# A 3x3 convolution with 2x2 max pooling on one core: the opening's order changed, one cast moved from ScalarE to VectorE

## The chip, the cores and the metric

The kernel runs on one core of one Trainium2 chip. The metric is the device time of one execution in microseconds (us); lower is better. Three executions of the kernel before took 104.12, 104.49 and 104.11 us, a median of 104.12 us. A core has five engines with a queue each: TensorE (PE, with its weight loads listed apart as PEld), VectorE (DVE), ScalarE (ACT), GpSimd (POOL) and SyncE (SP, which here only issues transfers). An engine takes its instructions strictly in the order of its own queue, and waits on semaphores for the others.

## The reference

The input x has 16 images of 64 channels, 64 by 64; the weight has 128 output channels. The convolution pads with one row and column of zeros; then the maximum of each 2x2 block is taken.

```python
x_pad = np.pad(x, ((0, 0), (0, 0), (1, 1), (1, 1)), mode='constant')
conv[b, co] += weight[co, ci, kh, kw] * x_pad[b, ci, kh:kh+64, kw:kw+64]   # over ci, kh, kw
output[b, c, i, j] = np.max(conv[b, c, 2*i:2*i+2, 2*j:2*j+2])              # 16 x 128 x 32 x 32, float32
```

## The kernel before, in words

**Tiling.** Two images make a pair: 2 x 64 channels fill the 128 partitions. Every pair is cut into 4 quarters of 16 input rows (8 output rows), which gives 32 steps. A step makes, for each of its two images (halves h = 0 and 1), one block of 128 output channels x 8 output rows x 64 columns. A product of 64 input channels uses half of the TensorE array, so two products, one on each half, run side by side; the kernel always issues them in such pairs (`product`, two lanes, L248).

**Algorithm.** The two convolution rows 2i and 2i+1 of a pooling window are not made one by one. With weight rows g0, g1, g2, one accumulator (`ta`) holds the part in which the two rows differ and another (`tb`) the part from which the maximum follows: VectorE takes the maximum of `tb` and the copied `ta` (MX, L427), and a last product that both rows share is added to it (PR for K steps, P1 for W steps). Each product is three matmuls, one for each column of the 3x3 window, onto one of eight PSUM banks.

**Two kinds of steps** (L37). K steps (0, 2, 5, 7, 10, ...) read the image as bf16 in `kx`. Their products are PA1 and PA2 (into `ta`), PB1 and PB2 (into `tb`) and PR (of `ks`, the sum of two rows, made on VectorE by KS, L296). W steps (1, 3, 4, 6, ...) read float32 rows in `wx`; GpSimd or VectorE makes the difference of two rows (E, L344) and the difference of rows one apart (D, L353), VectorE the sum (WS); products P2 (of E, into `ta`), P0 and P3 (of D), P1 (of WS). After the products ScalarE copies `ta` to SBUF (EV, L411 and L413), which frees the bank, VectorE takes MX, ScalarE copies odd columns (OD, L431), and VectorE takes the column maximum (CM, L437), which frees the `tb` bank; SP stores the result. For a W step, SE (L423) copies `ta` into the `tb` bank first.

**The opening.** SP loads, in this order: the weights; the first chunk of image pair 0 in two parts (`kfirst`); the rows of step 1 in two parts (`wx`); the chunk of step 2 (`ksecond`, L123). Weights are made as D0, D2, G0, G1, G2, GM and GP (`wq`), turned on TensorE by transposes (TD0 ... TGP, L164) and copied out of PSUM by VectorE or ScalarE (VD0 ... VGP, L175 to L181). The chunks of `kfirst` are cast to bf16 by VectorE (XEa, XOa, XOb, XEb, L453). The chunk of step 2 is cast by `cast_more` (L455): X1 casts the 8 rows 17, 19, ..., 31, X2 the 8 rows between them; both on ScalarE (L460), since `CAST_ON_VECTOR` is empty. PA1 and PA2 of step 2 read only odd rows, PB1 and PB2 only even rows, KS.2 all of them. The products of step 0 are cut in halves (F, products 0 to 3), those of step 1 too (G.k.part: G.0 the product P2, G.1 the product P0, G.2 the product P3), and the differences of step 1 are made in halves by VectorE (Ea, Eb) and GpSimd (Da, Db, L380).

**Chunks 3 and 4 of image pair 0** are loaded by GpSimd itself, cast by the DMA on the way: LK.0.0 (rows 33 to 48, read by step 5) and LK.0.1 (rows 49 to 63, read by step 7), both L98. They stand in GpSimd's queue in the order LK.0.0, Da, Db, LK.0.1, D.3, E.4, ...

**What sets the order.** The order is written out by hand, in the string `ORDER`; no scheduler moves anything. Every name in it appends its instructions to the queues of their engines. Beside the data dependencies there is one more rule (L76 to L82): a GpSimd operation made through `on_gpsimd` also waits for the last VectorE operation that was made through `on_vector` (casts, weight differences, KS, Ea and Eb) ahead of it in `ORDER`. LK.0.1 has no such wait of its own; it only stands behind what is ahead of it in GpSimd's queue. A PSUM bank is handed out from a queue of free ones, in the order of `ORDER`.

```python
def on_vector(inst):
    sbuf_op[0] = inst
    return inst

def on_gpsimd(inst):
    behind(inst, sbuf_op[0])
    return inst
```

Of the kernel before, what the change touches and what calls it, by code (L numbers as in the profile page):

```python
# [11 lines left out]
def kernel(  # L12
# [23 lines left out]

    TYPES = "KWKWWKWKWWKWWKWKWWKWWKWWWWKWWKWW"  # L37
    DIFF_ON_VECTOR = (3, 8, 14,)
    CAST_ON_VECTOR = ()
    SUM_BY_REDUCTION = (1, 3, 4, 11, 12, 14, 16, 17, 19, 20, 25, 30,)  # L40

    FROM_BANK = (6,)
# [33 lines left out]
# [3 lines that stand above are left out]
# [59 lines left out]
    D0, G2, D2, G0, G1, GM, GP = BLOCKS.values()  # L138
# [7 lines left out]
    g0, g1, g2 = wv[:, 0:3, :], wv[:, 3:6, :], wv[:, 6:9, :]  # L146
# [308 lines left out]
    def cast_more(first):  # L455
        dst, src = kx[0][:, klo2 + first : khi2 : 2, :], ksecond[:, first::2, :]
        if first in CAST_ON_VECTOR:
            on_vector(nc.vector.tensor_copy(out=dst, in_=src))
# [30 lines left out]
    for m in PRODUCTS:  # L489
        steps[m] = lambda s, h, m=m: product(m, s, h)  # L490

    ORDER = """
        D0 g2 TD0 g0 D2 GS TG2 g1 VD0 PR.0.1 XEa TD2 VG2 PA1.2.1 TG0 F.2.0 VD2 XOa LB.3 LB.4 LB.6 LB.8 LB.9 GM
        VG0 F.3.0 XOb F.0.0 F.1.0 TGM TG1 F.0.1 PA2.2.1 XEb LK.0.0 F.1.1 F.2.1 F.3.1 VGM GP Ea KS.0 Eb VG1
        EV.0.1 G.0.0 EV.0.0 G.0.1 P2.3.1 SE.1.0 SE.1.1 MX.0.1 Da Db TGP MX.0.0 VGP LK.0.1 X2 PR.0.0 G.1.0 X1
        G.2.0 PB1.2.1 PB2.2.1 WS.1 G.2.1 G.1.1 L.11 P0.3.1 PA1.2.0 PA2.2.0 P3.3.1 OD.0.0 OD.0.1 EV.1.0 E.3 KS.2
        CM.0.1 EV.1.1 P1.1.1 D.3 CM.0.0 PR.2.1 PB1.2.0 P2.3.0 PA1.5.1 PA2.5.1 MX.1.0 EV.2.0 MX.1.1 L.12 L.14
        WS.3 EV.2.1 E.4 SE.3.1 P1.1.0 PB2.2.0 SE.3.0 D.6 P2.4.1 OD.1.0 P0.3.0 MX.2.1 CM.1.0 EV.3.1 MX.2.0
        P3.3.0 PA1.5.0 EV.3.0 MX.3.1 WC.6 OD.1.1 D.4 MX.3.0 PA2.5.0 CM.1.1 PR.2.0 OD.2.1 P1.3.0 CM.2.1 E.6
# [91 lines left out]
```

## Time and profile before

| what | value |
|---|---|
| median of three executions | 104.12 us (104.11 to 104.49) |
| the profiled execution, its own time | 104.27 us |
| its span in the profile | 102.5 us, 2534 instructions |
| PE busy | 96.0 us (94%), 908 matmuls |
| DVE busy | 92.7 us (90%), 179 instructions |
| ACT busy | 81.5 us (80%), 180 instructions |
| POOL busy | 74.8 us (73%), 61 instructions |
| granted TensorE clock | 1.0 throughout |
| HBM traffic over the span | 17.14 MB read, 8.39 MB written |

The 104.27 us are the span and 1.77 us around it. Times below are in us from the span's start. An engine's busy share is an average over the span, and a matmul counts as busy until its modelled end, so that PE busy says little by itself; what counts is whether PE's matmuls follow each other without a gap, and what ended the gaps there are. In the view of the timeline a line is a run of like instructions: start, duration, engine, line, operation, tiles, shapes, count, and in brackets the idle time of the engine ahead of it and what ended it.

### The profile page before, as it was taken

How to read it: one execution, taken by the hardware profiler on the slowest of the kernel's cores; microseconds unless marked ns; L12 is line 12 of the kernel's file. 1: busy time of each engine (PE TensorE's matmuls, PEld its weight loads, DVE VectorE, ACT ScalarE, POOL GpSimd, SP SyncE). 2: the span in 40 equal slices, each digit the busy share in tenths (PEclk: the TensorE clock that was granted, in tenths of full speed). 3: DMA queues.
4: the chain of work that ended last, by engine and by line, in shares of the span. 5: the costliest groups of instructions: out<-in, count | busy, mean ns of one | idle time of the engine just before them, and what ended most of it. 6: DMA issues, size and time to landing. Idle time of an engine off the chain costs nothing.

```text
span 102.5 us, 2534 instructions
## 1 busy us (share of the span) xinstructions
PE 96.0 (94%) x908; PEld 55.7 (54%) x908; DVE 92.7 (90%) x179; ACT 81.5 (80%) x180; POOL 74.8 (73%) x61
## 2 busy tenths in 40 slices
PE   6889899999999999999999999999999999999920
PEld 2367655556865566566666667455444444444400
DVE  1497999999999899999999999999799899999970
ACT  5537988699699979978676999797898899897740
POOL 6128589997796889998999699668969967950000
PEclk9999999999999999999999999999999999999999
DMA  2999999999999999929999993023996522113244
GB/s 52 330 352 310 356 287 269 385 404 232 163 233 386 389 360 348 357 75 195 217 293 387 384 355 132 6 102 123 213 218 200 203 71 102 58 45 107 104 166 142
DMA packets 13421, 23.34 MB, mean 228 GB/s; under 512 B 1120, under 2 KB 9568, under 8 KB 13408
## 3 DMA queue, kind: packets, MB, share of 16 engines
q1 hardware_dynamic: 12400, 20.68, 59.4%
q0 software_dynamic: 864, 2.36, 13.3%
q8 instruction: 7, 0.11, 0.4%
q10 hardware_dynamic: 144, 0.13, 0.4%
q14 instruction: 6, 0.05, 0.1%
HBM read 17.14 MB, written 8.39 MB: 249 GB/s over the span
## 4 chain that ended last, share of the span: by engine, by line
PE 87%; DVE 5%; DMA 3%; issue 1%; DVEq 0%
PE acc L195 86%; DMA wraw<-in_weight_dram 3%; DVE acc L427 2%; DVE o L437 1%; PE acc L164 1%; DVE kx L453 1%; DVE wq L467 0%; DVE wt L181 0%; DVEq L586 0%; DVEq L427 0%
## 5 line engine op out<-in xcount | busy, mean ns | idle before, releaser
L195 PEld LDWEIGHTS <-wt 64*128 64x128 bf16 x876 | 53.3, 94 | 37.9 <-issue 1.8
L353 POOL TENSOR_TENSOR wd<-wx 128x1024 bf16<-128x1024 f32 x20 | 47.0, 2362 | 6.5 <-DVE ws L330 3.1
L195 PE MATMUL acc<-wd,wt 64*128 64x504 bf16 (+3 forms) x264 | 51.3, 367 | 0.0
L195 PE MATMUL acc<-kx,wt 64*128 64x504 bf16 (+6 forms) x288 | 48.5, 356 | 0.4 <-DVE kx L453 0.4
L427 DVE TENSOR_TENSOR acc<-acc,ev 128x512 f32<-128x512 f32 x64 | 41.8, 691 | 1.9 <-PE acc L195 0.8
L195 PE MATMUL acc<-we,wt 64*128 64x512 bf16 (+2 forms) x132 | 31.8, 367 | 0.0
L195 PE MATMUL acc<-ws,wt 64*128 64x504 bf16 (+1 forms) x126 | 30.7, 377 | 0.0
L413 ACT ACTIVATE ev<-acc 128x512 f32<-128x512 f32 x42 | 24.8, 605 | 3.6 <-PE acc L195 3.4
L423 ACT COPY acc<-acc 128x512 f32<-128x512 f32 x42 | 24.5, 589 | 3.8 <-PE acc L195 1.5
L431 ACT COPY od<-acc 128x256 f32<-128x256 f32 x64 | 22.8, 378 | 4.7 <-PE acc L195 4.4
L437 DVE TENSOR_TENSOR o<-acc,od 128x256 f32<-128x256 f32 x64 | 24.9, 414 | 1.0 <-ACT od L431 0.9
L344 POOL TENSOR_TENSOR we<-wx 128x512 bf16<-128x512 f32 x16 | 20.3, 1272 | 4.0 <-DVE ks L296 1.7
L195 PE MATMUL acc<-ks,wt 64*128 64x504 bf16 (+1 forms) x66 | 15.9, 377 | 0.5 <-DVE acc L427 0.5
L322 DVE TENSOR_REDUCE ws<-wx 128x512 bf16<-128x1024 f32 x12 | 14.7, 1229 | 0.0
L411 ACT COPY ev<-acc 128x512 f32<-128x512 f32 x22 | 12.4, 595 | 0.9 <-PE acc L195 0.8
L330 DVE TENSOR_TENSOR ws<-wx 128x512 bf16<-128x512 f32 x8 | 5.6, 708 | 0.0
L98 POOL DMA_DIRECT2D kx<-in_x_dram x6 | 3.5, 587 | 1.8 <-DVE kx L453 1.8
L296 DVE TENSOR_TENSOR ks<-kx 128x512 bf16<-128x512 bf16 x11 | 4.7, 442 | 0.0
L548 PE MATMUL acc<-const-bfloat16-1.0 128*128 128x512 bf16 x8 | 3.3, 585 | 0.8 <-PEq L572 0.8
L467 DVE TENSOR_TENSOR wq<-wraw 128x192 bf16<-128x192 f32 x1 | 0.5, 499 | 2.7 <-DMA wraw<-in_weight_dram 2.7
L380 POOL TENSOR_TENSOR wd<-wx 128x512 bf16<-128x512 f32 x2 | 2.5, 1262 | 0.5 <-DVE we L365 0.5
L468 POOL TENSOR_TENSOR gsum<-wraw 128x192 f32<-128x192 f32 x1 | 0.8, 812 | 2.7 <-DVE wq L466 2.7
(31 smaller groups left out, 21.9 us busy)
## 6 DMA issues: line engine op xcount, KB each, us to landing
out_dram<-o SPq DMA_DIRECT2D x26, 256.0 KB, 5.9
wx<-in_x_dram SPq DMA_DIRECT2D x10, 512.0 KB, 8.2
wx<-in_x_dram SPq DMA_DIRECT2D x5, 544.0 KB, 10.1
wx<-in_x_dram SPq DMA_DIRECT2D x5, 480.0 KB, 9.6
out_dram<-o SPq DMA_DIRECT2D x11, 128.0 KB, 2.0
kx<-in_x_dram POOLq DMA_DIRECT2D x2, 528.0 KB, 8.3
ksecond<-in_x_dram SPq DMA_DIRECT2D x1, 512.0 KB, 5.7
kx<-in_x_dram POOLq DMA_DIRECT2D x2, 256.0 KB, 8.4
```

What stands on the lines that cost most here:

```text
L195: nc.tensor.matmul(acc[t][:, i0:i1, o0:o1], wt[lo : lo + CI, m0 + kw - h, :], rows(lo, i0, i1, c0, c1), start=start and kw == 1, stop=True ...
L296: nc.vector.tensor_tensor(out=row["ks", s], in0=t[:, f : f + 2 * R : 2, :], in1=t[:, f + 1 : f + 2 * R : 2, :], op=ADD)
L322: nc.vector.tensor_reduce(out=row["ws", s], in_=t[:, f : f + 2 * R, :].rearrange("p (r two) w -> p r w two", two=2), axis=mybir.AxisListTy ...
L330: nc.vector.tensor_tensor(out=row["ws", s], in0=t[:, f : f + 2 * R : 2, :], in1=t[:, f + 1 : f + 2 * R : 2, :], op=ADD)
L344: inst = (nc.vector if vector else nc.gpsimd).tensor_tensor(out=row["we", s], in0=t[:, f : f + 2 * R : 2, :], in1=t[:, f + 1 : f + 2 * R : ...
L353: nc.gpsimd.tensor_tensor(out=row["wd", s], in0=t[:, f + 1 : f + 1 + 2 * R, :], in1=t[:, f - 1 : f - 1 + 2 * R, :], op=SUB)
L411: nc.scalar.copy(out=ev[s, h], in_=acc[t])
L413: nc.scalar.mul(ev[s, h], acc[t], -1.0)
L423: nc.scalar.copy(out=acc[t], in_=acc[ta[s, h]])
L427: nc.vector.tensor_tensor(out=t, in0=t, in1=ev[s, h], op=MAX)
L431: nc.scalar.copy(out=od[s, h], in_=acc[tb[s, h]][:, :, 1::2])
L437: nc.vector.tensor_tensor(out=ot[s][:, h], in0=acc[t][:, :, 0::2], in1=od[s, h], op=MAX)
```

## The change

Three things are changed, all in the opening.

1. `CAST_ON_VECTOR` becomes `(0,)`: X1 (odd rows of step 2's chunk) is issued on VectorE at L458 through `on_vector`, instead of on ScalarE. In `ORDER` it moves from behind G.1.0 to a place ahead of EV.0.1, and thus ahead of Da and Db. In VectorE's queue it stands behind VGP and ahead of MX.0.1. Da is now ordered behind X1, where it was ordered behind Eb.
2. The products PA1 and PA2 of step 2 (both halves) stand ahead of PR of step 0 in TensorE's queue. Before, they stood behind G.1 and G.2 of step 1. In the old string the half h = 1 of PR.0 stood first in its lane; the pairs themselves are the same ones.
3. TGP, the four transposes of GP, moves from behind G.0 to a place between F.2.1 and F.3.1; VGP moves with it on VectorE, from behind MX.0.0 to a place behind VG1.

With that TensorE's queue in the opening reads (before) F.3.1, G.0.0, G.0.1, TGP, PR.0, G.1.0, G.2.0, G.2.1, G.1.1, PA1.2, PA2.2, PB1.2.0 with P2.3.1, and (after) TGP, F.3.1, G.0.0, G.0.1, PA1.2, PA2.2, PR.0, G.1.0, G.2.0, G.1.1, G.2.1, PB1.2.0 with P2.3.1. From there on the order is the same. VectorE has one instruction more and ScalarE one less. The queues of GpSimd and SP hold the same instructions in the same order. The PSUM banks of some steps change places.

```diff
-    CAST_ON_VECTOR = ()
+    CAST_ON_VECTOR = (0,)
...
-        D0 g2 TD0 g0 D2 GS TG2 g1 VD0 PR.0.1 XEa TD2 VG2 PA1.2.1 TG0 F.2.0 VD2 XOa LB.3 LB.4 LB.6 LB.8 LB.9 GM
-        VG0 F.3.0 XOb F.0.0 F.1.0 TGM TG1 F.0.1 PA2.2.1 XEb LK.0.0 F.1.1 F.2.1 F.3.1 VGM GP Ea KS.0 Eb VG1
-        EV.0.1 G.0.0 EV.0.0 G.0.1 P2.3.1 SE.1.0 SE.1.1 MX.0.1 Da Db TGP MX.0.0 VGP LK.0.1 X2 PR.0.0 G.1.0 X1
-        G.2.0 PB1.2.1 PB2.2.1 WS.1 G.2.1 G.1.1 L.11 P0.3.1 PA1.2.0 PA2.2.0 P3.3.1 OD.0.0 OD.0.1 EV.1.0 E.3 KS.2
+        D0 g2 TD0 g0 D2 GS TG2 g1 VD0 XEa TD2 VG2 TG0 F.2.0 VD2 XOa LB.3 LB.4 LB.6 LB.8 LB.9 GM VG0 F.3.0 XOb
+        F.0.0 F.1.0 TGM TG1 F.0.1 XEb LK.0.0 GP F.1.1 F.2.1 TGP F.3.1 VGM Ea KS.0 Eb VG1 VGP X1 EV.0.1 G.0.0
+        EV.0.0 G.0.1 SE.1.0 SE.1.1 PA1.2.1 PA1.2.0 PA2.2.1 PA2.2.0 MX.0.1 Da Db MX.0.0 LK.0.1 PR.0.1 PR.0.0
+        P2.3.1 G.1.0 X2 G.2.0 PB1.2.1 PB2.2.1 WS.1 G.1.1 G.2.1 L.11 P0.3.1 P3.3.1 OD.0.0 OD.0.1 EV.1.0 E.3 KS.2
```

## The prediction

> **What bounds the kernel now.** I read the chain that ended last first. After an opening of about 10 us it is one piece of PE:
>
> ```profile
> 9.36 1.31 DVE acc L427 x2
> 10.67 0.04 issue
> 10.71 85.77 PE acc L195 x801
> ```
>
> 801 matmuls in 85.77 us, that is 0.214 us for each pair, the pace of a pair of 512 columns in the rows below. So from 10.71 us on PE hardly waits, and the end is PE's start plus its work plus a tail. Whatever delays PE after 10.71 us is paid in full; whatever starts it earlier is gained only if every operand comes earlier too. Next, PE's timeline in the opening and at step 7's first product:
>
> ```profile
> 7.76 1.49 PE L195 MATMUL acc<-kx,wt 64*128 64x256 bf16 x24
> 9.08 0.82 PE L195 MATMUL acc<-we,wt 64*128 64x256 bf16 x12
> 9.83 0.40 PE L164 MATMUL acc<-ident,wq 128*128 128x128 bf16 x4
> 10.71 0.82 PE L195 MATMUL acc<-ks,wt 64*128 64x512 bf16 x6 [0.48 <-DVE acc L427]
> 11.35 1.49 PE L195 MATMUL acc<-wd,wt 64*128 64x256 bf16 x24
> 12.67 1.67 PE L195 MATMUL acc<-kx,wt 64*128 64x512 bf16 x13
> ...
> 20.45 0.38 PE L195 MATMUL acc<-kx,wt 64*128 64x512 bf16 x1
> ```
>
> In order: the last half of F; G.0; TGP; PR.0 after a wait of 0.48 us for MX.0 (the only one that the change can remove); G.1 and G.2; PA1.2, PA2.2 and PB1.2.0; at 20.45 PA1.7.0. Third, the weight loads, which run ahead of their matmuls and so show waits that PE itself does not yet feel:
>
> ```profile
> 17.79 0.61 PEld L195 LDWEIGHTS <-wt 64*128 64x128 bf16 x8 [0.25 <-DMA kx<-in_x_dram]
> ...
> 20.32 0.69 PEld L195 LDWEIGHTS <-wt 64*128 64x128 bf16 x8 [0.19 <-DMA kx<-in_x_dram]
> ```
>
> Twice the load ahead of a matmul waits for an image transfer by GpSimd: at 17.79 for LK.0.0 (step 5), at 20.32 for LK.0.1 (step 7). The matmuls follow at 17.85 and 20.45, just on pace. Both transfers land with no slack. Fourth, GpSimd's timeline, which says when they are issued:
>
> ```profile
> 7.46 0.70 POOL L98 DMA_DIRECT2D kx<-in_x_dram  x1 [1.81 <-DVE kx L453]
> 8.65 2.50 POOL L380 TENSOR_TENSOR wd<-wx 128x512 bf16<-128x512 f32 x2 [0.50 <-DVE we L365]
> 11.10 0.57 POOL L98 DMA_DIRECT2D kx<-in_x_dram  x1
> 13.15 2.36 POOL L353 TENSOR_TENSOR wd<-wx 128x1024 bf16<-128x1024 f32 x1 [1.48 <-DVE ks L296]
> ```
>
> LK.0.0, then Da and Db, then LK.0.1, then D.3. The time from issue to landing of each, asked for L98 in a window around each issue, LK.0.0 first, LK.0.1 below:
>
> ```profile
> DMA to landing us min/median/max: 10.3/10.3/10.3
> ```
>
> ```profile
> DMA to landing us min/median/max: 9.2/9.2/9.2
> ```
>
> 7.46 + 10.3 = 17.76 and 11.10 + 9.2 = 20.3: the two edges at which PEld waits. Last, ScalarE:
>
> ```profile
> 10.94 1.15 ACT L460 CAST kx<-ksecond 128x512 bf16<-128x512 f32 x2
> 11.98 0.66 ACT L431 COPY od<-acc 128x256 f32<-128x256 f32 x2
> 12.86 1.08 ACT L413 ACTIVATE ev<-acc 128x512 f32<-128x512 f32 x2 [0.23 <-PE acc L195]
> ```
>
> EV.1.0 starts when PE has finished G.1; its end, 13.46, frees the bank that PB1.2.0 takes at 13.96.
>
> **Part 1, TGP and VGP ahead.** F takes 1.32 us for its last 24 matmuls (7.76 to 9.08), 0.33 a product. TGP stands ahead of the last of them and takes 0.33 to 0.40 us, 8.75 to 9.15. G.0 then runs 9.43 to 10.2, where TGP ended before: no work is saved, it changes places. VGP (0.41 us) runs 9.2 to 9.6 on VectorE, which idles from 8.83 to 9.36 before (0.53 us, for F). Cost nothing; the cover is that idle time.
>
> **Part 2, the cast X1 on VectorE.** It needs `ksecond`, issued at 3.08 and 5.7 us to landing: 8.8, in time. Its duration is not in the trace. The same line's kind on VectorE takes 0.28 us for 256 elements (L453), and 0.62 for 320 in its slowest case; ScalarE takes 0.63 for 512. A KS of 512 takes 0.42. Bounds 0.28 and 0.63; I take 0.41, twice the elements at the fast rows' growth. X1 runs 9.53 to 9.95. MX.0.1 and MX.0.0 (1.30 us) follow, 9.9 to 11.2 instead of 9.36 to 10.66. VectorE then has WS.1, E.3, KS.2 and CM.0 without a break, all 0.2 late; D.3, which waits for KS.2, ends at 15.7 instead of 15.51, and its product at 15.93 still finds it. The 0.2 mostly vanish in VectorE's idle 0.14 at 16.06. ScalarE loses 0.52 of work and X2 stays in time (11.3 to 11.9).
>
> **Part 3, A products ahead of PR.0.** They need X1 (9.95) at 10.2: no wait. Six pairs at 0.215 give 1.29: 11.5; PR.0, which needs MX.0 by then (11.2), runs to 12.13. So the 0.48 us at 10.23 is gone. What is late next: G.1 and G.2 now start at 12.13 instead of 11.35, G.1 is done at 13.3 instead of 12.83, EV.1.0 ends at 13.9 instead of 13.46, and PB1.2.0 can start at 13.95, against 13.45 where PE would be. Its bank gives the half microsecond back: PE stands where it stood, 13.96. SE.3.1, on ScalarE behind EV.1 and EV.2, ends about 0.15 later than 15.72, which may cost PE 0.05 at 15.93. And even if PE were early there, LK.0.0, issued at 7.46 as before, holds PA1.5.1 until 17.8. Gain of parts 1 to 3 at 17.85: 0 (bounds −0.5, if neither holds, and +0.1).
>
> **Part 4, the wait put on Da.** Da waited for Eb (8.56) and starts at 8.65; behind X1 it starts 0.09 after 9.95: 10.04, 1.39 later. Da and Db (2.50) end at 12.54. Their products are needed at 12.13 and 12.79 (halves at 11.30 and 12.54): no wait. Queued behind them on GpSimd is LK.0.1: issued at 12.49 instead of 11.10. D.3 behind it was waiting anyhow (1.48 us idle covers 1.39). SP's queue has nothing moved.
>
> LK.0.1 with its own 9.2 us lands at 21.69; in the case of LK.0.0 the matmul came 0.09 after landing, so PA1.7.0 starts at 21.78 against 20.45: PE stops for 1.33 us. The other end is no delay, if the DMA engines and not the issue set the landing: they are full (busy share 0.97 to 1.13 in each microsecond from 11 to 22), and LK.0.0's 256 KB are still under way at 12.5. With LK.0.0's 10.3 it would be 22.8, 2.4 us late. I take 1.33, for this is the same transfer in the same crowd: SP's queue holds load after load until 24 us, and from 14 to 16 us GpSimd's queue uses 27.8% of the engines, against 50.5% from 12 to 14 and 46.9% from 16 to 18: it runs dry between the two transfers, which speaks for an issue that decides.
>
> The Trainium skill speaks otherwise ("DMA: Bandwidth & Descriptors", section "Anatomy of one DMA"): a fixed cost of some 2 us plus bytes at 436 GB/s. By it 240 KB would be there about 2.6 us after issue (an estimate), near 15.1, and the delay would be hidden; the sum would be no change. The rows of 9.2 and 10.3 us in this trace disagree.
>
> **Sum.** 0 at 17.85, +1.33 at 20.45. PE runs without a gap from there before, so nothing is won back. The profiled execution took 104.27 (span 102.5 and 1.77 around it): 105.6. It stands 0.15 above the median of 104.12, so on the median 105.45; I say 105.4.
>
> **Rivals.**
> - The transfer is hidden anyway: LK.0.1 lands at 20.3, limited by the full engines. For it: their busy share, and LK.0.0 ahead in the same queue. Against: the dip from 14 to 16. Time 104.1 to 104.3 (parts 1 to 3).
> - Faster: the 0.48 us stay gained, 103.6. Place: PB1.2.0's bank at 13.45. It decides if EV.1.0 ends by 13.4, and then LK.0.0 would have to land 0.5 earlier than 17.76 and LK.0.1 not be late. Three rows speak against.
> - The crowd is worse: LK.0.1 takes 10.3 us or more, 22.8, PE stops 2.4 us: 106.5. For it: LK.0.0's row. Against: at 7.46 SP had just issued several loads together (6.35 to 9.38).
> - VectorE becomes the bound: 92.7 of 102.5 us busy, plus 0.41. Alone 104.5 at most; its idle times after 16 us cover it.
>
> **How the numbers follow.** LK.0.1 late by 0.6 to 1.7 us: 0.70, range of its own 104.8 to 105.9. Worse crowd 0.06. Hidden 0.15, VectorE alone 0.03. Faster 0.06. About 0.5% (0.52 us) is what a measurement tells from no change; so faster 0.06, same 0.18, slower 0.76. The range 104.1 to 106.0 leaves out the faster case and most of the worse crowd, about 0.12.
>
> **What would show it.** In the profile after: no wait of PE at 10.2; a wait of PE at 13.5 for L413 of about 0.5 us; L380 starting near 10.0 and the second L98 issue near 12.5; a wait of PE for the DMA `kx` near 20.5, of about 1.3 us, and the rest of the chain one piece of PE. Wrong if that second landing stays at 20.3, or if PE is early at 13.5 and stays so.

## The result and the profile after

The kernel after takes 104.55 us (median of 22 executions, 104.33 to 105.15), the kernel before 104.16 us beside it (22 executions, 104.01 to 104.92). The ratio is 1.0037, 95% interval [1.0021, 1.0053]: slower by 0.4 us, not by the 1.3 us forecast, and within the 0.5% that the prediction called the same. The profiled execution of after took 104.44 us, its span is 102.7 us. A quarter of the executions of after lie below 104.42 and a quarter above 104.90 (before: 104.11 and 104.37), so its upper part is more spread than its lower part is shifted; this comes up again below.

The middle of the chain that ended last, in the kernel after (start, us, what):

```profile
8.81 0.33 PE acc L164 x4
9.14 4.07 PE acc L195 x54
13.20 0.59 ACT ev L413
13.80 0.04 issue
13.84 82.86 PE acc L195 x759
```

The wait for MX.0 ahead of PR.0 is gone, and one for L413 (EV.1.0) stands in its place. PE's timeline shows the same, step by step:

```profile
10.06 1.46 PE L195 MATMUL acc<-kx,wt 64*128 64x512 bf16 x12
11.36 0.81 PE L195 MATMUL acc<-ks,wt 64*128 64x512 bf16 x6
12.01 1.48 PE L195 MATMUL acc<-wd,wt 64*128 64x256 bf16 x24
13.84 0.37 PE L195 MATMUL acc<-kx,wt 64*128 64x512 bf16 x1 [0.35 <-ACT ev L413]
...
20.32 0.38 PE L195 MATMUL acc<-kx,wt 64*128 64x512 bf16 x1
```

The six pairs, PR.0, G.1 and G.2 follow without a gap; PB1.2.0 starts at 13.84 (before: 13.96; this execution began its opening 0.11 us earlier, measured at the start of TGM's row, so PE stands where it stood). PA1.7.0, which was to stop for 1.33 us, runs at 20.32, on pace, and no weight load waits for an image transfer any more. GpSimd's timeline, then the time from issue to landing of the second transfer, LK.0.1:

```profile
10.03 2.50 POOL L380 TENSOR_TENSOR wd<-wx 128x512 bf16<-128x512 f32 x2 [2.00 <-DVE kx L458]
12.47 0.57 POOL L98 DMA_DIRECT2D kx<-in_x_dram  x1
```

```profile
DMA to landing us min/median/max: 7.4/7.4/7.4
```

LK.0.1 was issued 1.37 us later, as forecast (12.47 against 12.49 in the prediction), and landed at 19.9, earlier than before's 20.3. The loss is elsewhere. VectorE's timeline in after:

```profile
9.18 0.42 DVE L177 TENSOR_SCALAR wt<-acc 128x512 bf16<-128x512 bf16 x1 [0.40 <-PE acc L164]
9.52 0.42 DVE L458 CAST kx<-ksecond 128x512 bf16<-128x512 f32 x1
9.85 1.29 DVE L427 TENSOR_TENSOR acc<-acc,ev 128x512 f32<-128x512 f32 x2
11.05 1.23 DVE L322 TENSOR_REDUCE ws<-wx 128x512 bf16<-128x1024 f32 x1
12.19 0.88 DVE L344 TENSOR_TENSOR we<-wx 128x512 bf16<-128x512 f32 x1
13.00 0.41 DVE L296 TENSOR_TENSOR ks<-kx 128x512 bf16<-128x512 bf16 x1
...
16.34 0.68 DVE L427 TENSOR_TENSOR acc<-acc,ev 128x512 f32<-128x512 f32 x1
```

and the lines of before that answer to three of them:

```profile
12.05 0.67 DVE L344 TENSOR_TENSOR we<-wx 128x512 bf16<-128x512 f32 x1
12.64 0.41 DVE L296 TENSOR_TENSOR ks<-kx 128x512 bf16<-128x512 bf16 x1
...
16.20 0.70 DVE L427 TENSOR_TENSOR acc<-acc,ev 128x512 f32<-128x512 f32 x1
```

The two executions are best compared from the start of TGM's row (L164 x7: 7.26 before, 7.15 after). So counted, MX.0 is 0.60 us later (2.70 against 2.10), WS.1 0.27 (VGP's slot is no longer behind MX.0), KS.2 0.47 (E.3 took 0.88 us instead of 0.67), and the maximum at 16.34 still 0.25. Between KS.2 and that maximum it wins back 0.22 us: the idle time of 0.14 us at 16.06, and the 0.07 to 0.08 us by which instructions that follow each other without idle time overlap in these rows. From there VectorE has nowhere to catch up. The busy time of the engines in three stretches (columns: PE, PEld, DVE, ACT, POOL, the clock, the DMA share, GB/s), before:

```profile
10.00:16.00 6.00, 5.52 (x66) 3.65 (x65) 6.00 (x11) 5.56 (x12) 4.52 (x4) 1.00 1.05 316
16.00:25.00 9.00, 9.00 (x87) 4.82 (x85) 8.86 (x19) 7.55 (x18) 8.28 (x7) 1.00 1.05 338
25.00:33.00 8.00, 8.00 (x78) 5.71 (x76) 8.00 (x17) 6.70 (x17) 6.54 (x5) 1.00 1.02 248
```

and after:

```profile
10.00:16.00 6.00, 5.65 (x69) 3.39 (x64) 6.00 (x10) 5.05 (x11) 5.52 (x5) 1.00 1.04 350
16.00:25.00 9.00, 9.00 (x87) 7.48 (x87) 9.00 (x19) 7.62 (x18) 8.52 (x7) 1.00 1.01 324
25.00:33.00 8.00, 8.00 (x77) 4.20 (x75) 8.00 (x17) 6.57 (x16) 6.53 (x4) 1.00 1.03 222
```

DVE is busy 23 of 23 us in after, 22.86 before: the one idle time of 0.14 us is used up and 0.24 us of lateness remain. PE meets it later, in small waits. The first is at 15.91, for D.3 on GpSimd, which had waited for the late KS.2:

```profile
13.50 2.36 POOL L353 TENSOR_TENSOR wd<-wx 128x1024 bf16<-128x1024 f32 x1 [0.45 <-DVE ks L296]
```

```profile
15.91 0.37 PE L195 MATMUL acc<-wd,wt 64*128 64x512 bf16 x1
```

D.3 ends at 15.86 and its product starts 0.05 us later. Before, D.3 ended at 15.51, 0.42 us ahead of that product:

```profile
15.93 0.38 PE L195 MATMUL acc<-wd,wt 64*128 64x512 bf16 x1
```

The later ones show in the weight loads. Those of before in 14 to 44 us with idle time ahead of them, beside the two for image transfers that the prediction shows:

```profile
29.48 11.27 PEld L195 LDWEIGHTS <-wt 64*128 64x128 bf16 x107 [0.15 <-issue]
40.93 0.68 PEld L195 LDWEIGHTS <-wt 64*128 64x128 bf16 x8 [0.18 <-ACT acc L423]
41.77 2.25 PEld L195 LDWEIGHTS <-wt 64*128 64x128 bf16 x22 [0.16 <-issue]
```

and those of after:

```profile
25.66 3.58 PEld L195 LDWEIGHTS <-wt 64*128 64x128 bf16 x35 [0.15 <-issue]
29.48 6.16 PEld L195 LDWEIGHTS <-wt 64*128 64x128 bf16 x59 [0.24 <-issue]
35.83 4.99 PEld L195 LDWEIGHTS <-wt 64*128 64x128 bf16 x48 [0.19 <-ACT acc L423]
41.00 0.68 PEld L195 LDWEIGHTS <-wt 64*128 64x128 bf16 x8 [0.18 <-ACT acc L423]
41.89 0.36 PEld L195 LDWEIGHTS <-wt 64*128 64x128 bf16 x5 [0.21 <-issue]
42.49 1.60 PEld L195 LDWEIGHTS <-wt 64*128 64x128 bf16 x16 [0.24 <-issue]
```

At 25.66 the product of a W step starts 0.05 us after VectorE has ended the maximum (L427) that it adds to; before, the same matmul came 0.17 us after it, on PE's own pace. At 36.70, 41.89 and 42.48 a product again starts 0.05 us after such a maximum. The last two did so before too (41.77 and 42.37), so VectorE set PE's pace there already in the kernel before. At 29.48 it is a copy on ScalarE (L423), in before and after alike.

PE's matmuls run in two streams, one on each half of the array, and each stream keeps its own lateness. Counted as above and against before, one is 0.09 us late from 15.91 on, the other level (0.02 us early) up to 25 us. Both are 0.11 us late at 33, 0.23 at 45, and 0.32 at the last matmul (90.74 against 90.42). VectorE's idle times after 33 us do not win anything back: at 45 us it is still 0.23 us late, since by then what it waits for is late as well. The last 0.08 us come in one step at 77.70, behind maxima of VectorE that had waited 0.22 us at 76.1. That step is also in `m_before_late` below, which has the old order, and not in `n_after_late`, which has the new one; its cause stays open.

### The profile page after: what moved, and what is told of

Same layout as the page of the kernel before. It is cut to its first block, busy times and chain, and to the rows that moved or that the text cites. A ratio compares the mean times of both kernels' runs of the same rounds, so it can differ in the third digit from the quotient of the medians.

```text
span 102.7 us, 2535 instructions
## 1 busy us (share of the span) xinstructions
PE 97.1 (95%) x908; PEld 58.8 (57%) x908; DVE 93.0 (91%) x180; ACT 81.1 (79%) x179; POOL 74.9 (73%) x61
## 3 DMA queue, kind: packets, MB, share of 16 engines
HBM read 17.14 MB, written 8.39 MB: 249 GB/s over the span
## 4 chain that ended last, share of the span: by engine, by line
PE 93%; DVE 2%; ACT 1%; issue 0%; DVEq 0%
PE acc L195 87%; PE acc L548 3%; PE acc L164 2%; DVE o L437 1%; DVE acc L427 1%; ACT ev L413 1%; DVEq L586 0%
## 5 line engine op out<-in xcount | busy, mean ns | idle before, releaser
L195 PEld LDWEIGHTS <-wt 64*128 64x128 bf16 x876 | 55.8, 94 | 35.4 <-issue 2.2
L195 PE MATMUL acc<-wd,wt 64*128 64x504 bf16 (+3 forms) x264 | 51.3, 367 | 0.0
L195 PE MATMUL acc<-kx,wt 64*128 64x504 bf16 (+6 forms) x288 | 49.2, 356 | 0.4 <-ACT ev L413 0.4
L427 DVE TENSOR_TENSOR acc<-acc,ev 128x512 f32<-128x512 f32 x64 | 41.7, 689 | 1.3 <-ACT ev L413 0.7
L195 PE MATMUL acc<-we,wt 64*128 64x512 bf16 (+2 forms) x132 | 31.8, 367 | 0.0
L195 PE MATMUL acc<-ws,wt 64*128 64x504 bf16 (+1 forms) x126 | 30.9, 376 | 0.0
L423 ACT COPY acc<-acc 128x512 f32<-128x512 f32 x42 | 24.5, 590 | 4.5 <-PE acc L195 2.2
L413 ACT ACTIVATE ev<-acc 128x512 f32<-128x512 f32 x42 | 24.7, 605 | 3.5 <-PE acc L195 3.2
L195 PE MATMUL acc<-ks,wt 64*128 64x504 bf16 (+1 forms) x66 | 16.0, 377 | 0.0
L411 ACT COPY ev<-acc 128x512 f32<-128x512 f32 x22 | 12.4, 596 | 0.7 <-PE acc L195 0.5
```

The source lines that it names most:

```text
L195: nc.tensor.matmul(acc[t][:, i0:i1, o0:o1], wt[lo : lo + CI, m0 + kw - h, :], rows(lo, i0, i1, c0, c1), start=start and kw == 1, stop=True ...
L411: nc.scalar.copy(out=ev[s, h], in_=acc[t])
L413: nc.scalar.mul(ev[s, h], acc[t], -1.0)
L423: nc.scalar.copy(out=acc[t], in_=acc[ta[s, h]])
L427: nc.vector.tensor_tensor(out=t, in0=t, in1=ev[s, h], op=MAX)
```

## Experiments

All times are medians; "before" is the kernel before on the same chip.

**The load ahead of Da** (`a_load_first`), from the kernel after:

```diff
-MX.0.1 Da Db MX.0.0 LK.0.1 PR.0.1 PR.0.0
+MX.0.1 LK.0.1 Da Db MX.0.0 PR.0.1 PR.0.0
```

> The changed kernel, with LK.0.1 moved ahead of Da in GpSimd's queue: it is issued near 8.0 us instead of 12.47, while GpSimd waits for X1 anyway. Nothing else moves. Theory 1 (the late issue of LK.0.1 costs in those executions in which it then lands late): the median falls by 0.2 to 0.4 us to the time of before, 104.2, and the executions of 104.8 to 105.15 go. Theory 2 (LK.0.1 lands in time either way; what costs is VectorE and ScalarE, some tenths late at the tight places after 13 us): the time stays that of the changed kernel, 104.5, and so does its spread.

104.42 us (104.22 to 105.53) against 104.12, ratio 1.0043 [1.0018, 1.0069]. LK.0.1 was issued at 8.0, 4.4 us earlier than in after. The two transfers took 9.3 and 11.1 us, so LK.0.1 was there by 19.2 at the latest, against 19.9 in after, and PE's last matmul is as late as in after (0.31 us). A late LK.0.1 is not the cause.

**Da late in the kernel before** (`b_da_late`): the first half of D also waits for MX.0.1, as late as it is in after.

```diff
-        on_gpsimd(
+        inst = on_gpsimd(
...
+        if part == 0:
+            behind(inst, first_max[0])
```

> The kernel before, with one thing added: Da also waits for MX.0.1 on VectorE (ends 10.06), so that Da starts near 10.15 and LK.0.1 is issued near 12.6, as in the changed kernel; no cast and no product is moved. The prediction on record would give 105.4. Theory 1: above before by 0.3 to 0.4 us (104.5), with single executions near 105. Theory 2: at most 104.3; the only cost is E.3 on VectorE beside the later Db (0.88 us in the changed kernel, 0.67 before).

104.99 us (104.66 to 105.33) against 104.12, ratio 1.0076 [1.0049, 1.0103], between the theories and the 105.4 of the prediction. But not by LK.0.1, which was issued at 12.39, took 7.5 us and made PE wait nowhere near 20. In this order G.1 and G.2 come earlier than in after, so they met Da and Db themselves, and E.3 ran beside Db:

```profile
12.50 0.83 PE L195 MATMUL acc<-wd,wt 64*128 64x256 bf16 x12 [0.40 <-POOL wd L380]
```

```profile
11.85 1.14 DVE L344 TENSOR_TENSOR we<-wx 128x512 bf16<-128x512 f32 x1
```

As a copy of after's lateness the run is spoilt by that wait; of the transfer it says the same as the first.

**Da early in the kernel after** (`c_da_early`), with X1 beside Da and Db instead of ahead of them:

```diff
-VG1 VGP X1 EV.0.1 ... MX.0.1 Da Db MX.0.0 LK.0.1
+VG1 VGP Da Db LK.0.1 X1 EV.0.1 ... MX.0.1 MX.0.0
```

> The changed kernel, with Da, Db and LK.0.1 ahead of X1 in the order, so that Da waits for Eb again (starts near 8.6) and LK.0.1 is issued near 11.0; X1 then runs on VectorE beside Da. Theory 1: the time of before, 104.2. Theory 2: E.3 goes back to 0.67 us from 0.88, so VectorE is 0.2 us less late and part of the loss goes: 104.3 to 104.45. If X1 beside Da takes much longer than 0.42 us, PE waits for it at 10.2 and the time shows that too.

104.45 us (104.20 to 105.75) against 104.12, ratio 1.0051 [1.0020, 1.0083]. E.3 was back at 0.67 us, but X1 took 0.58 instead of 0.42, and VectorE was 0.21 us late all the same.

**X1 back on ScalarE, the rest as in after** (`d_x1_scalar`):

```diff
-    CAST_ON_VECTOR = (0,)
+    CAST_ON_VECTOR = ()
...
-VG1 VGP X1 EV.0.1 G.0.0 EV.0.0 G.0.1
+VG1 VGP EV.0.1 G.0.0 EV.0.0 X1 G.0.1
```

> The changed kernel without its cast on VectorE: X1 stays on ScalarE, but ahead of SE.1.0 (9.6 to 10.3). Da waits for Eb again, LK.0.1 is issued near 11.0, VectorE has MX.0 as early as F allows and E.3 no longer beside Db. PE waits some 0.1 us for X1 at 10.2. Theory 1: 104.2. Theory 2: VectorE is early by the cast and E.3, so that the loss after 13 us goes: 104.1 to 104.25, no faster, since PB1.2.0 still waits for the bank that EV.1.0 frees near 13.8.

104.42 us (104.15 to 104.76) against 104.12, ratio 1.0022 [1.0006, 1.0038]: above both forecasts. VectorE has less to do here, and is still 0.17 us late: the maximum MX.1.0 now waits for EV.1.0, which follows PE's G.1 behind the six pairs:

```profile
14.16 1.30 DVE L427 TENSOR_TENSOR acc<-acc,ev 128x512 f32<-128x512 f32 x2 [0.18 <-ACT ev L413]
```

So two things make VectorE late here by about the same: its own queue, and EV.1.0 late by the six pairs. Removing one leaves the other. In after MX.1.0 starts 0.21 us behind the end of EV.1.0.

**The kernel before with one cast more** (`e_extra_cast`), 512 elements, behind VGP, of which nothing is read:

```diff
+    def idle_cast():
+        nc.vector.tensor_copy(out=scratch, in_=kfirst[:, 0 : 2 * R : 2, :])
...
-MX.0.0 VGP LK.0.1
+MX.0.0 VGP XX LK.0.1
```

> The kernel before, with one cast of 512 elements more on VectorE (to a tile that nobody reads), between VGP and WS.1; nothing else moves. It makes VectorE 0.33 to 0.55 us late from WS.1 on, less its idle 0.14 at 16 us. Theory V (VectorE has no idle time from 10.6 to 33 us, so that its lateness is kept and PE pays it at its tight places after 25 us): 0.2 to 0.4 us above before, 104.3 to 104.5. Theory S (the loss of the changed kernel comes through ScalarE, which frees PB1.2.0's bank and copies SE.3.1 late): as before, 104.1.

104.80 us (104.31 to 105.27) against 104.16, ratio 1.0053 [1.0031, 1.0076]. Five of its 11 executions lie between 104.31 and 104.46, as expected, and six between 104.80 and 105.27, which no profile here explains. In its profile (104.40 us) VectorE is 0.24 us late, as late as in after, and PE's last matmul 0.24 us. PE's two streams become late in the same six places between 15.9 and 42.5 us as in after, and behind each of them they are as late as there within 0.02 us; the step at 77.7 is missing. The weight loads wait at places of after, though PE's order, the wait at PR.0 and Da, Db and LK.0.1 on GpSimd are those of before:

```profile
25.69 3.58 PEld L195 LDWEIGHTS <-wt 64*128 64x128 bf16 x35 [0.16 <-issue]
29.51 12.22 PEld L195 LDWEIGHTS <-wt 64*128 64x128 bf16 x115 [0.24 <-issue]
41.94 0.33 PEld L195 LDWEIGHTS <-wt 64*128 64x128 bf16 x5 [0.21 <-issue]
42.53 1.44 PEld L195 LDWEIGHTS <-wt 64*128 64x128 bf16 x15 [0.27 <-issue]
```

VectorE's lateness alone is enough for 0.24 of the 0.32 us that the profile of after loses.

**WS.1 by an addition instead of a reduction** in after (`f_after_ws1_add`) and in before (`g_before_ws1_add`), to give VectorE time back:

```diff
-    SUM_BY_REDUCTION = (1, 3, 4, 11, 12, 14, 16, 17, 19, 20, 25, 30,)
+    SUM_BY_REDUCTION = (3, 4, 11, 12, 14, 16, 17, 19, 20, 25, 30,)
```

> The changed kernel, with the row sum of step 1 (WS.1) made by an addition instead of a reduction: 0.68 to 0.9 us instead of 1.23, so that VectorE is 0.35 to 0.55 us less late from E.3 on. Theory V: the loss of 0.3 to 0.4 us goes, 104.1 to 104.25. Theory S: the time of the changed kernel, 104.5.

> The kernel before, with the same WS.1 by addition: VectorE is early by 0.35 to 0.55 us from E.3 on. Both theories: PE's first long piece starts at 10.7 all the same and is without a gap, so at most the short waits of PE go, 0.0 to 0.2 us: 103.95 to 104.15. Were VectorE the bound throughout, 103.7.

In after 104.93 us (104.71 to 105.11) against 104.16, ratio 1.0072 [1.0049, 1.0094]: the opposite of what I wanted. WS.1 took 0.80 us instead of 1.23, but as an addition it held up Db (1.71 us), and Db held up E.3, which had first waited 0.21 us for the rows of step 3:

```profile
12.21 1.47 DVE L344 TENSOR_TENSOR we<-wx 128x512 bf16<-128x512 f32 x1 [0.21 <-DMA wx<-in_x_dram]
```

```profile
10.18 2.94 POOL L380 TENSOR_TENSOR wd<-wx 128x512 bf16<-128x512 f32 x2 [1.98 <-DVE kx L458]
```

In before 104.34 us (104.07 to 104.66), ratio 1.0017 [1.0002, 1.0033]: no gain. MX.1.0 came 0.15 us earlier, but VectorE then idled 0.27 instead of 0.14 us at 16 us, and from the maximum behind that idle time on its positions and PE's are those of before to 0.01 us. Time saved ahead of it is not worth anything there.

**Half the products ahead** (`h_half_ahead`): as `c_da_early`, WS.1 by an addition, only PA1 ahead of PR.0, and PA2 behind G.2.

```diff
-PA1.2.1 PA1.2.0 PA2.2.1 PA2.2.0 MX.0.1 ... G.1.1 G.2.1
+PA1.2.1 PA1.2.0 MX.0.1 ... G.1.1 G.2.1 PA2.2.1 PA2.2.0
```

> The changed kernel with three things: Da, Db and LK.0.1 ahead of X1; WS.1 by addition; and only PA1 of step 2 ahead of PR.0, PA2 behind G.2 of step 1. G.1 is then done 0.65 us earlier and EV.1.0 frees its bank near 13.2, before PB1.2.0 can start at 13.4: the wait of 0.4 us at 13.8 goes and PE is 0.4 to 0.5 us early at 13.5. Theory V: PE keeps some 0.3 us of it, since VectorE is early by as much: 103.7 to 103.9. Theory S: the bank was all, 103.7. If LK.0.0 lands at 17.7 as in the profile of before, PE waits for it at 17.4 and half of the gain goes: 103.9 to 104.1.

104.70 us (104.20 to 105.85) against 104.16, ratio 1.0054 [1.0025, 1.0084]. Its profile is its second slowest execution (105.48 us). X1 started just behind the start of Db (9.65) and came out behind Db's end (10.91); the products waited for it:

```profile
9.67 1.53 DVE L458 CAST kx<-ksecond 128x512 bf16<-128x512 f32 x1
```

```profile
11.25 0.82 PE L195 MATMUL acc<-kx,wt 64*128 64x512 bf16 x6 [0.87 <-DVE kx L458]
```

**Part 1 alone** (`k_turn_only`), TGP and VGP moved, nothing else:

```diff
-F.1.1 F.2.1 F.3.1 VGM GP Ea KS.0 Eb VG1
+GP F.1.1 F.2.1 TGP F.3.1 VGM Ea KS.0 Eb VG1 VGP
```

> The kernel before with the first part of the change alone: TGP ahead of F.3.1 and VGP behind VG1; no cast moved, no product moved. The wait of PE at 10.2 for MX.0 stays. VectorE is 0.1 us early at WS.1. Theory W (what costs in the changed kernel's usual executions is part 3: G.1 later, so EV.1.0 later, so MX.1.0 later on a VectorE without idle time): as before, 104.05 to 104.2. If TGP ahead cost something by itself: 104.3 or more.

104.63 us (104.43 to 104.93) against 104.28, ratio 1.0034 [1.0017, 1.0050]. A part that I had costed at nothing costs 0.35 us when it stands alone. MX.0 waits for F.3.1, and TGP now runs ahead of F.3.1, so MX.0 comes 0.43 us later, counted from TGM's row, and PR.0 waits for it longer (0.48 us before):

```profile
11.05 0.82 PE L195 MATMUL acc<-ks,wt 64*128 64x512 bf16 x6 [0.81 <-DVE acc L427]
```

The rows of step 1 came late in this profile too (Ea waited 0.51 us for them), but MX.0 started 0.12 us behind the end of F.3.1, as in before (0.11), so it is F.3.1 that it waited for. In after the six pairs stand there and hide it.

**X1 on ScalarE and only PA1 ahead** (`i_one_ahead`, repeated as `o_one_ahead2`): `d_x1_scalar` with PA2 behind G.2 as in `h_half_ahead`.

```diff
-EV.0.0 X1 G.0.1 SE.1.0 SE.1.1 PA1.2.1 PA1.2.0 PA2.2.1 PA2.2.0 MX.0.1
+EV.0.0 X1 G.0.1 SE.1.0 SE.1.1 PA1.2.1 PA1.2.0 MX.0.1
...
-G.1.1 G.2.1
+G.1.1 G.2.1 PA2.2.1 PA2.2.0
```

> The changed kernel with X1 on ScalarE ahead of SE.1.0 (so Da waits for Eb, and E.3 on VectorE doesn't run beside Db), and with PA1 of step 2 alone ahead of PR.0, PA2 behind G.2. G.1 is done near 12.7, EV.1.0 near 13.3 and MX.1.0 starts near 13.6, as before; PE is 0.4 us early at 13.4. Theory W: the loss of 0.3 us goes, and no execution above 104.7 is left: 103.9 to 104.15. The prediction's own accounting (PE's start alone, waits for LK.0.0 aside): 103.7.

> The version with X1 on ScalarE, PA1 alone ahead of PR.0 and PA2 behind G.2, once more, with more executions (it took 104.08 us against 104.28 of the kernel before). If the gain is real: 103.9 to 104.1 us and the interval of the ratio below 1. If it was the scatter of late rows: within 0.1 us of the kernel before.

104.08 us against 104.28, ratio 0.9979 [0.9948, 1.0010], and 104.12 against 104.15, ratio 0.9994 [0.9977, 1.0011]. PE is 0.22 us ahead of before near 17.6 us and 0.21 up to 38, VectorE only 0.11 and 0.12, and the last matmul comes 0.04 and 0.03 us earlier. Between 38 and 43 us PE falls back to VectorE's lead, 0.10 and 0.12 us; the rest goes in the step near 77 us.

**The same with WS.1 by an addition** (`q_one_ahead_add`), where E.3 runs behind Db's end:

```diff
-    SUM_BY_REDUCTION = (1, 3, 4, 11, 12, 14, 16, 17, 19, 20, 25, 30,)
+    SUM_BY_REDUCTION = (3, 4, 11, 12, 14, 16, 17, 19, 20, 25, 30,)
```

> The same version with WS.1 by an addition instead of a reduction (0.85 us instead of 1.23 in the earlier run): VectorE has 0.4 us less to do before MX.1.0, which then waits for EV.1.0. Theory that VectorE's lateness after 10 us sets the rest: 103.7 to 103.95 us. If EV.1.0 sets MX.1.0 all the same: as without it, 103.95 to 104.1. If E.3, then earlier, meets Db on GpSimd (Db ends at 10.9, E.3 would start near 11.5): slower than that.

103.95 us (103.83 to 105.19) against 104.15, ratio 0.9996 [0.9973, 1.0019]. In the profile VectorE and PE are 0.21 us ahead near 17.6 us and the last matmul 0.12, which fits the lower median; the interval takes in no change. No version was shown to beat the kernel before.

**Two single executions of the kernel after** (`l_look1`, `l_look2`), for its executions above 104.7 us:

> The changed kernel again, for one look. Theory P (executions of 104.8 to 105.2 are those in which E.3 on VectorE is held up longer beside Db on GpSimd): an execution of 104.3 to 104.6 shows E.3 at 0.85 to 0.9 us, one above 104.8 shows it at 1.2 us or more. Otherwise E.3 is the same in both.

> The changed kernel once more, for a second look. Theory P as for the first look: 0.85 to 0.9 us for E.3 in an execution of 104.3 to 104.6, 1.2 us or more in one above 104.8.

They took 105.07 and 104.85 us. E.3 took 0.88 and 0.87 us, as in the execution of 104.44 (0.88), so my guess that E.3 makes the difference fell. What differs is that the rows of step 1 came late; in the first:

```profile
8.36 0.42 DVE L365 TENSOR_TENSOR we<-wx 128x256 bf16<-128x256 f32 x1 [0.81 <-DMA wx<-in_x_dram]
...
10.11 0.43 DVE L458 CAST kx<-ksecond 128x512 bf16<-128x512 f32 x1
```

In the second Ea waited 0.62 us, and TGM started 0.24 us later than in the execution of 104.44.

**Ea made late**, in before (`m_before_late`, shown) and after (`n_after_late`): two of the casts of `e_extra_cast` ahead of Ea.

```diff
-VGM GP Ea KS.0 Eb VG1
+VGM GP XX XX Ea KS.0 Eb VG1
```

> The kernel before, with two casts of 512 elements (to a tile nobody reads) on VectorE ahead of Ea: Ea, KS.0, Eb and VG1 come 0.67 us later (two steps of 0.34 us), as they do by themselves where the rows of step 1 land late (Ea waited 0.81 and 0.62 us for them in the two single looks at the kernel after, which took 105.07 and 104.85 us). Theory that lateness ahead of MX.0 is absorbed by VectorE's idle 0.53 us (8.83 to 9.36) in the kernel before: MX.0.1 starts some 0.1 us later only, 104.2 to 104.4 us. Rival, that such lateness costs both kernels the same: 104.6 to 104.8 us.

> The kernel after with the same two casts ahead of Ea. Theory that VGP and X1, put ahead of MX.0, have used up most of the idle time that covered late rows: idle 0.40 us ahead of VGP is left, so X1 and MX.0 come 0.25 to 0.35 us later, and PE pays it with its small waits: 104.7 to 104.9 us, and hardly any execution below 104.55. Rival, that the executions over 104.7 us of the kernel after come from E.3 beside Db and not from late rows: the usual time stays at 104.4 to 104.5 us, plus a spread as before.

Before with them: 104.37 us (104.22 to 104.70) against 104.15, ratio 1.0018 [0.9997, 1.0039], as expected. After with them: 104.59 us (104.51 to 104.90), ratio to before 1.0034 [1.0016, 1.0052]; expected were 104.7 to 104.9. The casts delay Ea by 0.83 and 0.78 us and cost both kernels a small amount: before some 0.2 us, while the ratio of after with them is no higher than without (1.0034 and 1.0037). That the change took away the cover for late rows is not shown. Why after's upper quarter is further up than before's stays open; late rows are seen in two slow executions of it, no more.

The run `n_after_late` also has the only profile in which LK.0.1 stopped PE, as the prediction had it. It was issued at 12.96 and took 8.1 us:

```profile
21.06 0.76 PEld L195 LDWEIGHTS <-wt 64*128 64x128 bf16 x10 [0.47 <-DMA kx<-in_x_dram]
```

One of PE's streams lost 0.34 us there and the other 0.14, but its last matmul is as late (0.52 us) as VectorE already was.

**All profiles in one table.** Times are counted from the start of TGM's row and given against the kernel before: a matmul near 17.6 us (the 740th from the end of L195, which lies in the stream that is level in after), the VectorE instruction with 149 behind it (in before the second maximum of the row at 17.14), and the last matmul.

| kernel | PE near 17.6 us | VectorE near 17.7 us | last matmul |
|---|---|---|---|
| `q_one_ahead_add` | −0.22 | −0.21 | −0.12 |
| `i_one_ahead` | −0.22 | −0.11 | −0.04 |
| `o_one_ahead2` | −0.22 | −0.12 | −0.03 |
| `g_before_ws1_add` | 0.00 | 0.00 | 0.00 |
| `d_x1_scalar` | +0.07 | +0.17 | +0.25 |
| `m_before_late` | +0.20 | +0.20 | +0.29 |
| `c_da_early` | +0.06 | +0.21 | +0.25 |
| `a_load_first` | −0.02 | +0.22 | +0.31 |
| after | −0.02 | +0.24 | +0.32 |
| `e_extra_cast` | 0.00 | +0.24 | +0.24 |
| `l_look2` | +0.03 | +0.38 | +0.45 |
| `k_turn_only` | +0.43 | +0.44 | +0.44 |
| `n_after_late` | +0.18 | +0.52 | +0.52 |
| `b_da_late` | +0.67 | +0.68 | +0.69 |
| `f_after_ws1_add` | +0.35 | +0.69 | +0.81 |
| `l_look1` | +0.41 | +0.74 | +0.83 |
| `h_half_ahead` | +1.05 | +1.06 | +1.16 |

The last column follows the third within 0.12 us, the second only within 0.46. PE can be level at 17.6 us and late at the end; in no row does it end earlier than VectorE's place says. The step of 0.08 us near 77 us is in all rows but before, `g_before_ws1_add`, `e_extra_cast`, `k_turn_only`, `n_after_late` and `b_da_late`.

## Why the prediction was wrong

**Part 4 failed.** Its step "LK.0.1 with its own 9.2 us lands at 21.69 … PE stops for 1.33 us" took the time from issue to landing of one execution for a property of the transfer. Issue at 8.0 gave a landing by 19.2, issue at 11.10 gave 20.3, at 12.39 and 12.47 gave 19.9, at 12.96 gave 21.0: the issue moves by 5 us, the landing by 2, and not in order. Over all profiles, nine issues between 10.8 and 11.3 landed between 18.8 and 20.3 (mean 19.5), six between 12.4 and 13.1 landed between 19.9 and 21.0 (mean 20.3). So the landing moved by 0.8 us on average for 1.8 us of issue, and at like issue it scatters by 1.5 us from execution to execution. The bound that I named and did not take, that the full DMA engines set the landing, is what the runs speak for (their share is 1.04 in after between 10 and 16 us); no run has emptier engines, so this is not shown. The dip of GpSimd's queue between 14 and 16 us, on which I chose, did not decide. The estimate of 2.6 us from the Trainium skill ("DMA: Bandwidth & Descriptors", section "Anatomy of one DMA") gave the right outcome, a hidden transfer, and a wrong duration: 7.2 us and more in every profile.

**Part 2 failed by a smaller sum, and this is the loss.** X1 took 0.42 us (0.41 forecast) and MX.0 started at 9.85 (9.9). VectorE was to be 0.2 us late, and that was to "mostly vanish" in its idle 0.14 us. It was 0.27 us late at WS.1 and 0.47 by KS.2, because E.3 took 0.88 instead of 0.67 us beside Db: Da had been moved by X1, and I asked only who needs Da's result and not which VectorE instruction would now run beside it. The idle time took 0.22 of it, and 0.24 stayed. The step on D.3, that "its product at 15.93 still finds it", failed with it: D.3 ended at 15.86, not 15.7, and the product waited.

**The rival that came true** was "VectorE becomes the bound", with its 104.5 at most against 104.55 measured, to which I gave 0.03. I set it aside with the words "its idle times after 16 us cover it". They don't: up to 33 us there is only that 0.14, and by 43 us PE has waited and, having no gaps, never wins it back. In the median 0.39 us were lost; VectorE's lateness is shown for 0.24 of the 0.32 us in the profile, and the step near 77 us and the wider upper part of the executions stay open. The chain of waits shows PE alone for 85 us because PE's waits are then 0.1 us each, and each matmul is shown busy for 0.38 us while the next of its stream starts 0.215 us behind it: so small a wait leaves no gap, and a second engine with as little room does not appear in the chain.

**Part 3 was right for PE.** The wait of 0.48 us went, G.1 and EV.1.0 came later, and PB1.2.0 waited 0.35 us for EV.1.0 at 13.84 (forecast: about half a microsecond at 13.5, start at 13.95); PE stood where it had stood. `i_one_ahead`, with three pairs ahead instead of six, has no such wait and is 0.22 us ahead there. It left VectorE out: EV.1.0, late by the six pairs, holds MX.1.0, so that VectorE stays 0.17 us late even where X1 is on ScalarE (`d_x1_scalar`).

**Part 1 was right only in company.** TGP and VGP cost PE nothing visible with the six pairs behind them (no run has the pairs without them), and 0.35 us without the pairs. I had checked PE's work and VectorE's idle time for VGP, not that MX.0 waits for the F product that TGP is put ahead of.

## What to carry to other kernels

Where one engine runs without a gap, ask which other engine has none either in the stretch behind the change: the busy time by windows shows it where the average of the whole span and the chain of waits don't, and what is added there comes out at the end almost in full, up to tens of microseconds later and in waits too small for the lists (0.24 us in `e_extra_cast`). The time from issue to landing of one transfer, read from a trace whose DMA engines are full (here 1.04), must not be added to a new issue time. When an operation of GpSimd is moved, look at what VectorE does beside it in its new place.

## What the runs showed of the hardware

E.3 (a subtraction of two operands in SBUF, 0.67 us alone) and the casts (0.42 us) were held up beside Da or Db on GpSimd (1.26 us each), and each time to the same point: E.3 ended 0.55, 0.55 and 0.54 us after the GpSimd operation ended (after, `f_after_ws1_add`, `b_da_late`), however early it had started, which made it 0.88, 1.47 and 1.14 us long; the cast ended 0.28, 0.28 and 0.29 us after it (`h_half_ahead`, `c_da_early`, `e_extra_cast`), 1.53, 0.58 and 0.53 us long. It goes both ways: Db ended 1.13 us after the VectorE instruction that it had met, in `f_after_ws1_add` (WS.1's addition; Db took 1.71 us) and in `c_da_early` (X1; 1.45 us). WS.1 as a reduction took 1.22 to 1.24 us in every profile, also where Db ran beside it (after, `b_da_late`). This agrees with the Trainium skill ("SBUF — State Buffer", section "Who interferes with whom"): a VectorE instruction with two SBUF inputs, or a cast in a fast mode, and a GpSimd operation that reads SBUF exclude each other for a whole instruction, and a `tensor_reduce` does not take part.

Second, the two transfers of 240 and 256 KB issued by GpSimd into full DMA engines took 7.2 to 11.1 us over all profiles, and one of them landed earlier in after than in before though it was issued 1.37 us later.
